# Depthwise-convolution taps, channel sums and buffer places rearranged in a one-core layer kernel

## The chip, the cores and the metric

One Trainium2 chip; the kernel runs on 1 core. The metric is the device time of one execution in microseconds. Before the change it is 2488.69 us, the median of 3 runs (2487.4 to 2490.93). TensorE (PE) multiplies, VectorE (DVE), ScalarE (ACT) and GpSimd (POOL) work on elements, SyncE (SP) issues most of the DMAs. PE takes weights and data from SBUF and writes to PSUM, which has eight banks of 128 x 512 floats here.

## The reference

One layer on 512 positions of width 2048, all in fp32. Two mixers share one normalised input h, then a gated merge and a small embedding step:

```
proj = h @ w_in                       # qkv, z_a, b, a, glu_in, z_b, gate_logits
o_a  = gated_delta(silu(conv4(qkv)))  # 16 heads of 128, chunks of 64: a triangular solve per chunk
y_a  = (rmsnorm(o_a) * silu(z_a)) @ w_br_a
u    = glu(glu_in)                    # first half * sigmoid(second half)
u    = causal_depthwise_conv(u, w_dw) + b_dw            # 31 taps for each of 2048 channels
y_b  = (silu(layernorm(u)) * silu(z_b)) @ w_br_b        # mean and variance over the channels
x    = x + rmsnorm((sigmoid(ga) * y_a + sigmoid(gb) * y_b) @ w_out)
x    = x + rmsnorm(sigmoid(x @ w_ple_gate) * (p @ w_ple_proj))
```

## The kernel before, in words

**Products.** Each fp32 operand is split into a high part (a cast, on ACT) and a low part (the difference, on DVE or POOL), and a product is three matmuls: high by high, high by low, low by high. A matmul here is 128 x 128 by 128 x 512. A weight piece is read from memory by SP into a raw tile (three buffers), cast (L126) and subtracted (L127) into a tile of the pool `ring` (four buffers, low in each SBUF partition). `low_part[0]` names the engine of L127: DVE at first, POOL from the end of the heads until the layer norm begins.

**Stages, in order of time.** The input is loaded, normalised and transposed. `z_phase` makes z and both gates with a Strassen-Winograd scheme: sums of weight blocks are formed by DVE and by accumulating DMAs that POOL issues, and the pieces (L404 to L414) lie by turns in `ring` and, every third, in two tiles of the pool `slots` (21 buffers of 2 KB, high in the partition). Then the heads: eight groups of two, each with six products for q, k and v (`gemm_cm`, 48 matmuls each at L183, L185, L187, with two PSUM banks in turn), then the gated delta rule, of which the last steps are a triangular solve on DVE (a product L846 and a reduction L847 in turn) and small matmuls (L748, L867) that wait for it. Then branch a (L1052, L1054, L1056 with oh and ol) alternates with the products of the gated linear unit: for each of the channel tiles 5 to 15 two products of 48 matmuls, and after each pair from 6 on a job of 48 matmuls of branch a. The layer norm over the channels follows beside the last jobs of branch a, then branch b (L1052 again, with uh and ul), then w_out by Strassen-Winograd (L1341 to L1343), and the embedding step.

**Background work.** Every matmul of `gemm_cm` and `branch` calls `tick()`. Generators are spawned with a period in ticks and step when it has passed: `group` for a head group, `convs` for the depthwise convolution, `split_oa` for the low parts `ol` of branch a (L1031), `layer_norm`. The order on each engine is fixed before the run by a scheduler that goes through the program with its own costs: an instruction is issued when its operands are ready and the buffer of its tile is free by those costs, the one that stands first in the program ahead of the others. Buffers of one tag are given in program order. On the chip each engine keeps to that order, and an instruction that has to wait holds up all behind it on its engine.

**The convolution.** For a tile of 128 channels `evac_glu_b` puts a sigmoid into the tile `sg`; `evac_glu_a` multiplies the other half of the unit by it (L943). Up to the end of the heads, channels 0 to 4, the product stays in `sg` (SBUF); after it a PSUM pool `ups` of two banks is open, and the product is written there (`up`). `dwconv` starts the sum of a channel on ACT (L919, `uc`) and does 30 taps on DVE (L922), one for each step of the generator, with period CP = 4. When they are done, POOL adds the channel to `acc` (L926, L928; its mean over channels opens the layer norm), and SP writes it to memory (L929). `convs` is spawned 288 matmuls before the end of the heads.

**w_out.** `run` takes two PSUM banks for each product from `bank()`: six of eight calls give one from the pool `fps` (f), two one from `gps` (g). The operands of w_out are formed at the same time by `split_mixed`, whose transposed tiles also lie in `gps` and are read last at L1225. With the counter at 0, P1, P7 and the second P1 get f f, f f, f g, and P2 g f.

Of the kernel before, what the change touches and what calls it, by code (L numbers as in the profile page):

```python
# [24 lines left out]
TAPS = 31  # L25
LOP = 23
HP = 4
CP = 4
QKV_TILES = 48
Z_TILE0 = 48  # L30
BA_TILE = 64
# [6 lines left out]
V_DW = V_CONV + QKV_TILES * 4  # L38
V_BDW = V_DW + NK * TAPS
# [41 lines left out]
def _body(ctx, tc, A, out):  # L81
    nc = tc.nc
# [25 lines left out]
    def vv(col, n=1):  # L108
        return vec[:, col:col + n]
# [31 lines left out]
    def spawn(gen, period, key=None):  # L141
        active.append([gen, period, period, key])
# [147 lines left out]
    B11, B12, B22, B21 = range(4)  # L290
    OPND = {"P1": "A11", "Q5": "S1", "P7": "S3", "P6": "S2", "P3": "S4", "P2": "A12", "Q4": "A22"}

    def stepper(gen, n=1):
        def f(k=None):
            for _ in range(n):
                next(gen, None)
        return f

    def z_phase():
        ctx_z = ExitStack()  # L300
        zs = ctx_z.enter_context(tc.tile_pool(name="zs", bufs=32))
        zps = ctx_z.enter_context(tc.tile_pool(name="zps", bufs=6, space=PSUM))
        S = {n: [None] * 4 for n in ("S1", "S2", "S3", "S4")}

        def tt_(dst, a, b, op):
            nc.vector.tensor_tensor(dst, a, b, op)
# [42 lines left out]
        WZ = {g: A["w_" + g] for g in ("z", "ga", "gb")}  # L349
        entries, sources, pieces = deque(), deque(), deque()  # L350
        tz = {}
        cnt = dict(load=0, piece=0)

        def load(grp, jp, blk, q):
            cnt["load"] += 1
            if cnt["load"] <= 4 or cnt["load"] % 5 in (2, 4):
                two = [slots.tile([P, T], F32, tag="s", name="zraw") for _ in range(2)]
                for n in range(2):
                    nc.sync.dma_start(two[n], WZ[grp][jp, blk, q][:, n * T:(n + 1) * T])
                return two  # L360
            raw = rawp.tile([P, 1024], F32, tag="raw", name="raw", bufs=3)
            nc.sync.dma_start(raw, WZ[grp][jp, blk, q])
            return [raw[:, 0:T], raw[:, T:]]

        def acc(t, grp, jp, blk, q):
            nc.gpsimd.dma_start(t, WZ[grp][jp, blk, q], accum_op=ALU.add)

        def parts(t):
            return [t[:, 0:T], t[:, T:]]

        def e_a(grp, jp, q):
            b11, b12 = load(grp, jp, B11, q), load(grp, jp, B12, q)
            tz[q] = zs.tile([P, 1024], F32, tag="t", name="zt", bufs=4)
            t = parts(tz[q])
            for n in range(2):
                tt_(t[n], b11[n], b12[n], ALU.add)
            return [b11, t]

        def e_b(grp, jp, q):
            b22, b12 = load(grp, jp, B22, q), load(grp, jp, B12, q)  # L380
            t = parts(tz[q])
            for n in range(2):
                tt_(t[n], t[n], b22[n], ALU.add)
                tt_(b12[n], b12[n], b22[n], ALU.add)
            return [t, b12, b22]

        def e_c(grp, jp, q):
            acc(tz[q], grp, jp, B21, q)
            return [load(grp, jp, B21, q), parts(tz[q])]

        for grp in WZ:
            for jp in range(2):
# [3 lines left out]
        def enter():  # L396
            e, *where = entries.popleft()
            for src in e(*where):
                sources.extend(src)

        def piece():
            while len(pieces) < 4 and (sources or entries):
                while len(sources) < 4 and entries:
                    enter()  # L404
                src = sources.popleft()
                cnt["piece"] += 1
                if cnt["piece"] % 3:
                    w = ring.tile([P, 1024], F32R, tag="w", name="w")
                    hi, lo = w[:, 0:T], w[:, T:]
                else:  # L410
                    hi, lo = [slots.tile([P, T], F32R, tag="s", name="zw") for _ in range(2)]
                nc.scalar.copy(hi, src)
                tt_(lo, src, hi.bitcast(F32), ALU.subtract)
                pieces.append((hi, lo))  # L414
            return pieces.popleft()

        def run(products, side=None):
            ps = {pr: [zps.tile([P, T], F32, tag="z", name="zp") for _ in range(2)] for pr in products}
            for q in range(4):
                for pr in products:  # L420
                    for n in range(2):
                        wh, wl = piece()
                        for t in range(2):
                            lh, ll = opnd(OPND[pr], 2 * q + n, t)
                            mm(ps[pr][t], lh, wh, start=q + n == 0, stop=False)  # L425
                            mm(ps[pr][t], ll, wh, start=False, stop=False)  # L426
                            mm(ps[pr][t], lh, wl, start=False, stop=q == 3 and n == 1)  # L427
                    if side:
                        side()
            return ps  # L430
# [22 lines left out]
        gen = form()  # L453
# [7 lines left out]
        for grp, jp in [(g, n) for g in WZ for n in range(2)]:  # L461
            rows = None if grp == "z" else bias_rows(grp, jp)
            ps = run(("P1", "Q5"), stepper(gen, 2))
# [8 lines left out]
            ps = run(("P6", "P7", "P3"))  # L472
# [11 lines left out]
            ps = run(("P2", "Q4"))  # L484
# [45 lines left out]
    u_dram = dram.tile([NK, P, T], F32, name="u_dram")  # L530
# [374 lines left out]
    cpool = [slots, "s"]  # L905
    ups = None
    waiting = deque()
# [5 lines left out]
            sg_t[i] = sg  # L913
        return f

    def dwconv(i, u):
        w0 = V_DW + i * TAPS
        y = cpool[0].tile([P, T], F32, tag=cpool[1], name="uc")
        nc.scalar.activation(y, u, AF.Identity, scale=vv(w0 + TAPS - 1), bias=vv(V_BDW + i))  # L919
        yield  # L920
        for s in range(1, TAPS):
            nc.vector.scalar_tensor_tensor(y[:, s:], u[:, 0:T - s], vv(w0 + TAPS - 1 - s), y[:, s:], ALU.mult, ALU.add)  # L922
            yield
        if i == 0:
            acc.append(slots.tile([P, T], F32, tag="s", name="acc"))
            nc.gpsimd.tensor_copy(acc[0], y)  # L926
        else:
            nc.gpsimd.tensor_tensor(acc[0], acc[0], y, ALU.add)  # L928
        nc.sync.dma_start(u_dram[i], y)  # L929
        done[0] += 1  # L930

    def convs():
        while done[0] < NK:
            if waiting:
                yield from dwconv(*waiting.popleft())
            else:
                yield

    def evac_glu_a(i):
        def f(ps):  # L940
            sg = sg_t.pop(i)
            u = ups.tile([P, T], F32, tag="u", name="up") if ups else sg
            nc.vector.tensor_tensor(u, ps, sg, ALU.mult)  # L943
            waiting.append((i, u))
        return f

    def glu_b(i):
# [57 lines left out]

    jobs.append(lambda: spawn(convs(), CP, "convs"))
    for i in range(2, 5):
# [10 lines left out]
    ups = s2_ctx.enter_context(tc.tile_pool(name="ups", bufs=2, space=PSUM))  # L1018
# [278 lines left out]
    def load(jp, pr, q):  # L1297
        n = loads[0]
        loads[0] += 1
        if n < 3 or n % 8 in (1, 4, 7):  # L1300
            raw = rawp.tile([P, 1024], F32, tag="raw", name="raw", bufs=3)
        else:
            raw = s3.tile([P, 1024], F32, tag="rw", name="rw", bufs=5)
        src, blk = WHICH[pr]
        nc.sync.dma_start(raw, src[jp, blk, q])
        sources.append(raw)
# [35 lines left out]
            mm(ps, ll, wh[:, c], start=False, stop=False)  # L1342
            mm(ps, lh, wl[:, c], start=False, stop=kk == 7)  # L1343

    banks = [0]

    def bank():
        banks[0] += 1
# [99 lines left out]
    fin = out_fin(0, gp)  # L1448
    ps = run(("P7",), stepper(gen, 2))
    s7 = [snap(SLOT, x) for x in ps["P7"]]  # L1450
    ps = run(("P1",), stepper(gen, 3))
    drain(gen)
    s1b = [snap(HP_, x) for x in ps["P1"]]
    ps = run(("P2",))
    for t in range(2):
        fin(t, 0, add(unit(S3_, "c11"), ps["P2"][t], s1[t]))
    ps = run(("Q5",))
    s5 = [snap(S3_, x) for x in ps["Q5"]]
    ps = run(("P6",))
# [28 lines left out]
    ps = run(("P7",), stepper(pgen))  # L1488
# [5 lines left out]
    ps = run(("Q4",), stepper(pgen, 3))  # L1494
# [81 lines left out]
    last = ple_last(bcast_row(A["g_ple"], 3))  # L1576
    for k in range(12, NK):
        hold(k)
    for tt in range(NTT):
        ps = bank()  # L1580
# [8 lines left out]
        for j in range(4):  # L1589
            s = e_t4[tt][j]  # L1590
# [67 lines left out]
```

## Time and profile before

| what | value |
|---|---|
| median of 3 runs | 2488.69 us (2487.4 to 2490.93) |
| the profiled execution | 2491.45 us, its span 2489.7 us |
| PE busy | 2431.6 us, 98% of the span |
| DVE, ACT, POOL busy | 1821.3, 1160.2, 426.5 us |
| mean granted clock of PE | 0.991 |
| head stage | some 590 to 1520 us |
| last tap of the convolution | ends at 1904.6 us |
| branch b, first matmul | 1949.96 us |

How to read it: an engine's busy time counts its instructions, not its waits. A wait of an engine is put down to the instruction that released it: "PE g L187 <- POOL w L127: 14.0, 1, 14.0" says that the matmul at L187 waited 14.0 us in total, once, 14.0 at most, until POOL's L127 had written w. Rows of a timeline give start, length, engine, line, operation, output and inputs, count, and in brackets the idle time ahead with what ended it. Groups give the count, the sum of busy time in us and the mean of one in ns. Matmuls overlap in the records, so their pitch is the distance between two starts. Stretches of 50 us give each engine's busy time in us and count, the granted clock of PE (1.00 is full), the share of time in which the DMA engines worked, and GB/s.

### The profile page before, as it was taken

What the parts mean: (1) busy time and instruction counts of PE and PEld (TensorE: products, weight loads), DVE (VectorE), ACT (ScalarE), POOL (GpSimd) and SP (SyncE); (2) the same over time, 40 slices, a digit from 0 to 9 for tenths busy, and PEclk for the clock granted to TensorE, in tenths of its full rate; (3) what the DMA queues carried; (4) which work ended last, traced back from release to release, by engine and by line L of the source; (5) the groups of instructions that cost most, each with busy time, mean ns of one, the idle gap of its engine ahead of it and who ended that gap; (6) DMA issues with size and microseconds to landing.
All of it is one profiled execution on the core that took longest, in us unless ns stands there. A gap on an engine that the chain in (4) does not pass through costs nothing. (4 is left out here: it accounts for less than half of the span.)

```text
span 2489.7 us, 33469 instructions
## 1 busy us (share of the span) xinstructions
PE 2431.6 (98%) x11962; PEld 1989.3 (80%) x11962; DVE 1821.3 (73%) x3401; ACT 1160.2 (47%) x2284; POOL 426.5 (17%) x451
## 2 busy tenths in 40 slices
PE   8999999999999999999999989799999999999998
PEld 7888888887888888888888867688888788788886
DVE  7878787877677676777767799978777854667644
ACT  6445444555555555555565534122223623444532
POOL 0000000012212112132200114445553000000000
PEclk9999999999999999999999999899999999999999
DMA  7567675766636354475622224233344543575542
GB/s 266 169 183 206 183 206 195 227 163 188 185 110 185 102 158 129 130 204 151 181 75 93 73 85 141 84 102 106 108 139 135 182 127 98 186 235 170 204 169 76
DMA packets 141831, 380.19 MB, mean 153 GB/s; under 512 B 15968, under 2 KB 24416, under 8 KB 141664
## 3 DMA queue, kind: packets, MB, share of 16 engines
q1 hardware_dynamic: 119008, 319.32, 38.5%
q0 software_dynamic: 20352, 54.54, 9.9%
q10 hardware_dynamic: 2304, 4.20, 0.5%
q8 instruction: 94, 1.54, 0.3%
q14 instruction: 73, 0.60, 0.1%
HBM read 329.75 MB, written 48.23 MB: 152 GB/s over the span
## 5 line engine op out<-in xcount | busy, mean ns | idle before, releaser
L126 ACT CAST w<-raw 128x512 fp32r<-128x512 f32 x588 | 359.1, 619 | 587.2 <-PE g L187 272.1
L187 PE MATMUL g<-hh,w 128*128 128x512 f32 x1536 | 611.4, 398 | 16.1 <-POOL w L127 14.0
L183 PE MATMUL g<-hh,w 128*128 128x512 f32 x1536 | 610.4, 397 | 2.8 <-DVE up L943 1.6
L185 PE MATMUL g<-hl,w 128*128 128x512 f32 x1536 | 611.4, 398 | 0.0
L127 DVE TENSOR_TENSOR w<-raw,w 128x512 fp32r<-128x512 f32 x444 | 307.3, 699 | 170.6 <-ACT w L126 168.3
L187 PEld LDWEIGHTS g<-hh,w 128*128 128x128 f32 x1536 | 289.8, 189 | 73.3 <-POOL w L127 14.4
L183 PEld LDWEIGHTS g<-hh,w 128*128 128x128 f32 x1536 | 289.9, 189 | 57.9 <-ACT w L126 3.0
L185 PEld LDWEIGHTS g<-hl,w 128*128 128x128 f32 x1536 | 289.8, 189 | 56.1 <-issue 1.5
L922 DVE SCALAR_TENSOR_TENSOR uc<-up,vec,uc 128x505 f32<-128x505 f32 (+18 forms) x330 | 233.2, 731 | 52.8 <-ACT uc L919 45.5
L127 POOL TENSOR_TENSOR w<-raw,w 128x512 fp32r<-128x512 f32 x144 | 193.9, 1349 | 221.4 <-ACT w L126 216.2
L922 DVE SCALAR_TENSOR_TENSOR uc<-sg,vec,uc 128x508 f32<-128x508 f32 (+20 forms) x150 | 128.2, 881 | 0.6
L660 DVE SCALAR_TENSOR_TENSOR cv<-g,vec,cv 128x511 f32<-128x511 f32 x144 | 106.3, 738 | 27.3 <-ACT cv L658 26.8
L1052 PE MATMUL yp<-w,uh 128*128 128x512 f32 x256 | 101.3, 396 | 4.6 <-ACT uh L1140 4.6
L1056 PE MATMUL yp<-w,ul 128*128 128x512 f32 x256 | 101.1, 396 | 0.0
L1054 PE MATMUL yp<-w,uh 128*128 128x512 f32 x256 | 101.0, 395 | 0.0
L426 PE MATMUL zp<-w,zol 128*128 128x512 f32 x256 | 100.4, 392 | 0.0
L1054 PE MATMUL yp<-w,oh 128*128 128x512 f32 x256 | 99.7, 390 | 0.5 <-POOL w L127 0.5
L1052 PE MATMUL yp<-w,oh 128*128 128x512 f32 x256 | 100.1, 391 | 0.0
L425 PE MATMUL zp<-w,zoh 128*128 128x512 f32 x256 | 99.9, 390 | 0.0
L427 PE MATMUL zp<-w,zoh 128*128 128x512 f32 x256 | 99.7, 389 | 0.0
L1056 PE MATMUL yp<-w,ol 128*128 128x512 f32 x256 | 99.6, 389 | 0.0
L846 DVE TENSOR_TENSOR prod<-UT,VT 128x2 f32<-128x2 f32 (+30 forms) x248 | 87.7, 354 | 5.8
(384 smaller groups left out, 4713.9 us busy)
## 6 DMA issues: line engine op xcount, KB each, us to landing
raw<-in_w_in SPq DMA_DIRECT2D x194, 512.0 KB, 3.4
wsum<-in_w_out POOLq DMA_DIRECT2D x96, 256.0 KB, 5.1
raw<-in_w_ple_gate SPq DMA_DIRECT2D x40, 512.0 KB, 4.2
wo_sums<-wsum POOLq DMA_DIRECT2D x64, 256.0 KB, 4.0
raw<-in_w_br_a SPq DMA_DIRECT2D x32, 512.0 KB, 3.3
raw<-in_w_br_b SPq DMA_DIRECT2D x32, 512.0 KB, 3.3
raw<-in_w_ga SPq DMA_DIRECT2D x24, 512.0 KB, 4.4
raw<-in_w_gb SPq DMA_DIRECT2D x24, 512.0 KB, 4.4
```

Source lines behind the costliest of these rows:

```text
L126: nc.scalar.copy(hi, rq)
L127: low_part[0].tensor_tensor(lo, rq, hi.bitcast(F32), ALU.subtract)
L183: mm(ps, wh, rh, start=(k == 0), stop=False)
L185: mm(ps, wh, rl, start=False, stop=False)
L187: mm(ps, wl, rh, start=False, stop=(k == NK - 1))
L425: mm(ps[pr][t], lh, wh, start=q + n == 0, stop=False)
L426: mm(ps[pr][t], ll, wh, start=False, stop=False)
L660: nc.vector.scalar_tensor_tensor(y[:, s:], ps[:, 0:T - s], vv(w0 + 3 - s), y[:, s:], ALU.mult, ALU.add)
L922: nc.vector.scalar_tensor_tensor(y[:, s:], u[:, 0:T - s], vv(w0 + TAPS - 1 - s), y[:, s:], ALU.mult, ALU.add)
L1052: mm(ps[tt], lh[:, b], wh, start=k == 0, stop=False)
L1054: mm(ps[tt], lh[:, b], wl, start=False, stop=False)
L1056: mm(ps[tt], ll[:, b], wh, start=False, stop=k == NK - 1)
```

## The change

Four things change.

- The convolution. Its period before the heads end is 10 ticks for a tap instead of 4; once `ups` is open a tap takes 3 and 4 ticks in turn. The product of the linear unit always goes into `sg` in SBUF. `near()` prepares the next channel at tap 24 of the current one: once `ups` is open it copies the product to a PSUM tile on ACT, and it starts the sum on ACT. The channel's addition to `acc` is written at tap 18 of the next channel (`filtered`), its DMA to memory stays behind its last tap.
- The block sums `zt` of the z phase move from four tiles of 4 KB in the pool `zs` to eight of 2 KB in `slots`, with two accumulating DMAs of 256 KB in place of each of 512 KB.
- Weight pieces of the z phase lie by turns in `ring` and in a new pool `zw` of four buffers, opened ahead of `zs`, low in the partition; none lies in `slots`.
- In w_out the bank counter starts at -1: P1, P7 and the second P1 get f f, P2 gets g g. The operands' generator is stepped with 2 instead of 3 during the second P1.

```diff
-CP = 4
+CP = 10
...
+        zw = ctx_z.enter_context(tc.tile_pool(name="zw", bufs=4))
         zs = ctx_z.enter_context(tc.tile_pool(name="zs", bufs=32))
...
         def acc(t, grp, jp, blk, q):
-            nc.gpsimd.dma_start(t, WZ[grp][jp, blk, q], accum_op=ALU.add)
+            for n in range(2):
+                nc.gpsimd.dma_start(t[n], WZ[grp][jp, blk, q][:, n * T:(n + 1) * T], accum_op=ALU.add)
...
-            tz[q] = zs.tile([P, 1024], F32, tag="t", name="zt", bufs=4)
-            t = parts(tz[q])
+            t = tz[q] = [slots.tile([P, T], F32, tag="s", name="zt") for _ in range(2)]
...
-                if cnt["piece"] % 3:
-                    w = ring.tile([P, 1024], F32R, tag="w", name="w")
-                    hi, lo = w[:, 0:T], w[:, T:]
-                else:
-                    hi, lo = [slots.tile([P, T], F32R, tag="s", name="zw") for _ in range(2)]
+                w = ring.tile([P, 1024], F32R, tag="w", name="w") if cnt["piece"] % 2 else zw.tile([P, 1024], F32R, tag="zw", name="zw")
+                hi, lo = w[:, 0:T], w[:, T:]
...
+    def filtered(i, y):
         if i == 0:
             acc.append(slots.tile([P, T], F32, tag="s", name="acc"))
             nc.gpsimd.tensor_copy(acc[0], y)
         else:
             nc.gpsimd.tensor_tensor(acc[0], acc[0], y, ALU.add)
-        nc.sync.dma_start(u_dram[i], y)
         done[0] += 1
 
+    def near():
+        if not waiting:
+            return None
+        i, u = waiting.popleft()
+        if ups:
+            up = ups.tile([P, T], F32, tag="u", name="up")
+            nc.scalar.copy(up, u)
+            u = up
+        y = cpool[0].tile([P, T], F32, tag=cpool[1], name="uc")
+        nc.scalar.activation(y, u, AF.Identity, scale=vv(V_DW + i * TAPS + TAPS - 1), bias=vv(V_BDW + i))
+        return i, u, y
+
+    def pace(s):
+        return (3 + s % 2) if ups else CP
+
     def convs():
+        ready = last = None
         while done[0] < NK:
-            if waiting:
-                yield from dwconv(*waiting.popleft())
-            else:
-                yield
+            ready = ready or near()
+            if not ready:
+                if last and last[0] == NK - 1:
+                    filtered(*last)
+                yield 1
+                continue
+            (i, u, y), ready = ready, None
+            w0 = V_DW + i * TAPS
+            for s in range(1, TAPS):
+                nc.vector.scalar_tensor_tensor(y[:, s:], u[:, 0:T - s], vv(w0 + TAPS - 1 - s), y[:, s:], ALU.mult, ALU.add)
+                if s == 18 and last:
+                    filtered(*last)
+                    last = None
+                if s == 24:
+                    ready = near()
+                yield pace(s)
+            nc.sync.dma_start(u_dram[i], y)
+            last = i, y
...
-            u = ups.tile([P, T], F32, tag="u", name="up") if ups else sg
-            nc.vector.tensor_tensor(u, ps, sg, ALU.mult)
-            waiting.append((i, u))
+            nc.vector.tensor_tensor(sg, ps, sg, ALU.mult)
+            waiting.append((i, sg))
...
-    banks = [0]
+    banks = [-1]
...
-    ps = run(("P1",), stepper(gen, 3))
+    ps = run(("P1",), stepper(gen, 2))
     drain(gen)
```

More of the change, by code (lines that the diff above doesn't have):

```diff
@@ L365, in acc @@
         def acc(t, grp, jp, blk, q):
-            nc.gpsimd.dma_start(t, WZ[grp][jp, blk, q], accum_op=ALU.add)
-        def parts(t):
-            return [t[:, 0:T], t[:, T:]]
+            for n in range(2):
+                nc.gpsimd.dma_start(t[n], WZ[grp][jp, blk, q][:, n * T:(n + 1) * T], accum_op=ALU.add)
         def e_a(grp, jp, q):
             b11, b12 = load(grp, jp, B11, q), load(grp, jp, B12, q)
-            tz[q] = zs.tile([P, 1024], F32, tag="t", name="zt", bufs=4)
-            t = parts(tz[q])
+            t = tz[q] = [slots.tile([P, T], F32, tag="s", name="zt") for _ in range(2)]
             for n in range(2):
@@ L380, in e_b @@
             b22, b12 = load(grp, jp, B22, q), load(grp, jp, B12, q)
-            t = parts(tz[q])
+            t = tz[q]
             for n in range(2):
@@ L388, in e_c @@
             acc(tz[q], grp, jp, B21, q)
-            return [load(grp, jp, B21, q), parts(tz[q])]
+            return [load(grp, jp, B21, q), tz[q]]
         for grp in WZ:
@@ L914, in evac_glu_b @@
         return f
[L916 to L919, printed above, removed]
-        yield
-        for s in range(1, TAPS):
-            nc.vector.scalar_tensor_tensor(y[:, s:], u[:, 0:T - s], vv(w0 + TAPS - 1 - s), y[:, s:], ALU.mult, ALU.add)
-            yield
+    def filtered(i, y):
         if i == 0:
@@ L928, in dwconv @@
             nc.gpsimd.tensor_tensor(acc[0], acc[0], y, ALU.add)
-        nc.sync.dma_start(u_dram[i], y)
         done[0] += 1
+    def near():
[11 more added lines that the diff above has]
+        return (3 + s % 2) if ups else CP
     def convs():
+        ready = last = None
         while done[0] < NK:
-            if waiting:
-                yield from dwconv(*waiting.popleft())
-            else:
-                yield
+            ready = ready or near()
[16 more added lines that the diff above has]
+            last = i, y
     def evac_glu_a(i):
```

## The prediction, made before the changed kernel was run

> **What bounds the kernel now.** I read the page's first part, then what TensorE (PE) waited for, then the 50-us stretches around each wait, and the rows of the engine named.
>
> ```profile
> PE 2431.6 (98%) x11962; PEld 1989.3 (80%) x11962; DVE 1821.3 (73%) x3401; ACT 1160.2 (47%) x2284; POOL 426.5 (17%) x451
> ```
>
> PE is busy for 98% of the span and the change takes no matmul away. So only three things can be won: PE's waits, time at a lowered clock, and the pitch of a matmul. The waits of PE that touch the change (total, times, longest, us):
>
> ```profile
> PE g L187 <- POOL w L127: 14.0, 1, 14.0
> PE py L867 <- DVE Tc L861: 4.9, 1, 4.9
> PE yp L1052 <- ACT uh L1140: 4.6, 1, 4.6
> PE f L1341 <- DVE sf L1225: 4.4, 1, 4.4
> PE po L748 <- DVE O L743: 2.5, 2, 1.4
> PE g L183 <- DVE up L943: 1.6, 1, 1.6
> ```
>
> The stretches that hold them (busy time and count of PE, weight load, DVE, ACT, POOL; granted clock; DMA share; GB/s):
>
> ```profile
> 1450.00:1500.00 50.00, 43.19 (x267) 32.64 (x266) 44.70 (x91) 18.96 (x43) 7.46 (x5) 0.90 0.22 69
> 1550.00:1600.00 50.00, 35.98 (x153) 29.40 (x152) 49.82 (x59) 9.18 (x15) 20.55 (x14) 0.87 0.25 85
> 1900.00:1950.00 50.00, 45.20 (x200) 36.20 (x198) 37.65 (x65) 23.66 (x39) 8.18 (x7) 0.99 0.44 149
> 1950.00:2000.00 50.00, 50.00 (x210) 40.70 (x211) 40.09 (x67) 26.90 (x45) 0.00 (x0) 0.95 0.48 162
> 2150.00:2200.00 50.00, 45.55 (x193) 37.04 (x192) 33.34 (x43) 27.13 (x37) 0.00 (x0) 0.93 0.64 220
> ```
>
> A wait of 4.4 us or more is followed by a lowered clock. One minus the clock, times 50 us, is what it costs beyond the wait: 5.0, 6.5, 0.5 + 2.5 = 3.0, and 3.5 us. With it the four places cost 9.9, 20.5, 7.6 and 7.9 us.
>
> **Why GpSimd (POOL) is late by 14 us.** From the heads' end on it makes the weights' low parts (L127) and adds each convolved channel to the sum (L928). Its rows, then DVE's for the taps, and DVE's groups, the first two of them in 1520 to 1650 us:
>
> ```profile
> 1593.59 1.68 POOL L928 TENSOR_TENSOR acc<-acc,uc 128x512 f32<-128x512 f32 x1 [19.90 <-DVE uc L922]
> ```
> ```profile
> 1553.55 18.72 DVE L922 SCALAR_TENSOR_TENSOR uc<-sg,vec,uc 128x507 f32<-128x507 f32 x17
> 1572.79 26.30 DVE L922 SCALAR_TENSOR_TENSOR uc<-sg,vec,uc 128x497 f32<-128x497 f32 x35
> 1604.55 19.91 DVE L922 SCALAR_TENSOR_TENSOR uc<-up,vec,uc 128x507 f32<-128x507 f32 x26
> ...
> L922 DVE SCALAR_TENSOR_TENSOR uc<-sg,vec,uc 128x491 f32<-128x491 f32 (+22 forms) x70 | 66.4, 1000 | 0.2
> L922 DVE SCALAR_TENSOR_TENSOR uc<-up,vec,uc 128x511 f32<-128x511 f32 (+29 forms) x60 | 44.0, 733 | 2.3 <-ACT uc L919 0.4
> L1031 DVE TENSOR_TENSOR ol<-oa,oh 128x512 fp32r<-128x512 f32 x16 | 14.6, 915 | 0.0
> L943 DVE TENSOR_TENSOR up<-g,sg 128x512 f32<-128x512 f32 x11 | 7.6, 691 | 1.3 <-PE g L187 1.1
> ```
>
> The sum stands at the head of POOL's queue and waits 19.9 us for a tap, with low parts behind it. PE got 19.9 − 14.0 = 5.9 us further on pieces already prepared. The taps are late because one that reads u from SBUF (sg) while POOL works comes every 18.72/17 = 1.10 us; with POOL quiet every 26.30/35 = 0.75; from PSUM (up) every 19.91/26 = 0.77 with POOL at work. The excess is 70 × (1.000 − 0.733) = 18.7 us, and 16 × (0.915 − 0.691) = 3.6 us for the low parts ol: 22.3, about the 19.9 seen.
>
> The Trainium skill agrees ("SBUF — State Buffer", section "SBUF: two separate sides"): a DVE operation with two SBUF inputs and a GpSimd one that reads SBUF exclude each other for a whole instruction. A rule speaks against the change: "VectorE: DVE Perf Modes", "Rules for kernel authors", advises a copy from PSUM to SBUF where many operations follow, and this kernel will do the opposite. By it the copies would only cost; the rows, 0.75 quiet from SBUF against 0.77 from PSUM, leave it nothing to save and show it 0.33 worse beside POOL.
>
> **The parts, with gains positive.**
>
> *Sums and taps.* Channels 2 to 15 will be read from PSUM, so of 70 stretched taps at most channel 1's 30 remain: 30 × 0.267 + 3.6 = 11.6 us, scaled by 19.9/22.3 to 10.4, less the 5.9 of cover: a wait of 4.5 and some 3.4 of clock, together 8 at worst; nothing if that channel is done before POOL takes the low parts. That the sum is written a channel later I count as nothing: where the scheduler issues an operation as soon as it thinks it ready, its place in the queue stays. I take half, 4: gain 20.5 − 4 = **16.5** (0 if the queue is as before, to 20.5). The accumulation per channel and its DMA stay one each.
>
> *The copies to PSUM.* 14 more on ACT, with a cast as the nearest row:
>
> ```profile
> L126 ACT CAST w<-raw 128x512 fp32r<-128x512 f32 x588 | 359.1, 619 | 587.2 <-PE g L187 272.1 <-PE yp L1056 203.6 <-PE f L1509 42.5
> L919 ACT ACTIVATE uc<-up,vec 128x512 f32<-128x512 f32 x11 | 8.5, 782 | 0.3 <-DVE up L943 0.3
> ```
>
> 14 × 0.62 = 8.7 us, hidden: ACT is busy for 47% of the span, and for 9.2 of 50 us in the stretch from 1550. A copy waits for the PSUM buffer of the channel before last, and weight casts queue behind it; it is issued 24 taps after that buffer's last reader, so 24 × 0.77 = 18 us of lateness are covered. Without the cover each costs 0.6. The GLU product no longer waits for such a buffer: the 1.6 us at L943, which held PE's bank, go: **1.6** (0 to 2.5).
>
> *Sparse taps before the heads' end.* A tap per 10 matmuls, not 4. It is not the pace alone that places them:
>
> ```profile
> 1419.22 0.15 DVE L846 TENSOR_TENSOR prod<-UT,VT 128x2 f32<-128x2 f32 x1
> 1419.29 0.73 DVE L922 SCALAR_TENSOR_TENSOR uc<-sg,vec,uc 128x499 f32<-128x499 f32 x1
> 1419.95 0.15 DVE L847 TENSOR_REDUCE VT<-prod 128x1 f32<-128x2 f32 x1
> ...
> 1438.51 0.28 DVE L846 TENSOR_TENSOR prod<-UT,VT 128x60 f32<-128x60 f32 x1
> 1438.82 0.22 DVE L847 TENSOR_REDUCE VT<-prod 128x4 f32<-128x60 f32 x1
> ```
>
> Taps fill each gap of the last solve, and stretch a product-to-reduce step from 0.31 to 0.73 us. If all went, the waits at L867 and L748 would: 9.9 + 2.5 = 12.4. But channel 0 is ready as before, and only channel 1, whose start I expect some 8 us later in a solve of about 30 us from there, thins out: a quarter, **3** (−3, if SBUF slots run short, to 12.4).
>
> *Layer norm.* Its end of the chain:
>
> ```profile
> 1857.05 9.32 DVE L922 SCALAR_TENSOR_TENSOR uc<-up,vec,uc 128x511 f32<-128x511 f32 x12 [9.09 <-ACT uc L919]
> 1866.29 0.69 DVE L943 TENSOR_TENSOR up<-g,sg 128x512 f32<-128x512 f32 x1
> 1866.88 27.28 DVE L922 SCALAR_TENSOR_TENSOR uc<-up,vec,uc 128x499 f32<-128x499 f32 x41
> 1899.31 5.26 DVE L922 SCALAR_TENSOR_TENSOR uc<-up,vec,uc 128x488 f32<-128x488 f32 x7
> 1949.96 0.79 PE yp L1052
> ```
>
> The last tap ends at 1904.57, and branch b starts 45.4 us later, 4.6 after PE was ready for it (1945.4). Channel 15's product comes at 1866.3, when 18 taps of channel 14 are still to do; at 30 × 3.5 = 105 matmuls a channel against 144 between products, channel 14 will be done. Then copy 0.6, start 0.8 and 30 × 0.77 = 23 put the last tap 25 us after the product instead of 38: 13 us won against 4.6 missing. Gain **7.6** (−10 to 7.6, the third rival).
>
> *z and gates.* Start-to-start of 6 matmuls on a piece in two high tiles (zw), then 12 on ring pieces:
>
> ```profile
> 304.40 0.39 PE L425 MATMUL zp<-zw,hh 128*128 128x512 f32 x1
> 305.80 0.39 PE L425 MATMUL zp<-w,hh 128*128 128x512 f32 x1
> 308.54 0.39 PE L425 MATMUL zp<-zw,hh 128*128 128x512 f32 x1
> ```
>
> 233 against 228 ns; 3 × 128 + 3 × 96 = 672 such matmuls: **3.4** (0, if the pitch isn't the address's, to 3.4). The block sums now take eight of the 21 slots, in which loads and results of this stage live too, and each accumulating DMA becomes two on POOL's queue, which works at nothing else there: 24 issues more. One row of the page gives a load's time to landing:
>
> ```profile
> raw<-in_w_ga SPq DMA_DIRECT2D x24, 512.0 KB, 4.4
> ```
>
> No wait of PE in this stage is over 1 us, so loads are ahead; a load that found no slot could cost its 4.4 us once, which would turn the 3.4 into −1.
>
> *w_out's banks.*
>
> ```profile
> 2163.54 0.39 PE L1343 MATMUL f<-wsp,ah 128*128 128x512 f32 x1
> 2168.38 0.77 PE L1341 MATMUL f<-wsp,ah 128*128 128x512 f32 x1 [4.45 <-DVE sf L1225]
> ...
> 2167.81 0.76 DVE L1225 TENSOR_TENSOR sf<-tp,sf 128x256 f32<-128x256 f32 x2
> ```
>
> The second half of P1 waits for a bank that L1225 still reads. With both banks in the other pool, 24 matmuls × 0.227 = 5.4 us can run before P2 needs it; it was short by 4.45, so 0.95 is to spare. The mix's steps come closer together (every second call, not every third), but two weight splits of 1.22 each could now come ahead of L1225:
>
> ```profile
> 2158.37 1.22 DVE L1323 TENSOR_TENSOR wsp<-rw,wsp 128x1024 fp32r<-128x1024 f32 x1 [0.82 <-ACT wsp L1322]
> ```
>
> That would leave 1.5 us of wait, too short to lower the clock; I take off half. Gain 7.9 − 0.8 = **7.1** (0, where P2 waits instead, to 7.9).
>
> Sum: 16.5 + 1.6 + 3 + 7.6 + 3.4 + 7.1 = 39.2. The profiled run took 2491.45 (span 2489.7, 1.75 around it), so 2452.3; the median shown is 2.8 lower: 2449.5, **2450 us**. Its own range, 2441 to 2459, is the widest term's way to its end (heads, 9.4) to either side.
>
> **Rivals.** *Heads freed:* the solve runs without taps and POOL never waits: 9.4 + 4 more, **2436**. For: taps visibly stretch the solve. Against: channel 0's are ready all the same. *POOL waits as before:* the sum keeps its place and channel 1 is as late: 2450 + 16.5 = **2466**. Against: 40 of 70 stretched taps go. *DVE is full:* with some 40 taps done by the heads' end (1520.7 − 6.4 = 1514.3), 440 remain, and 14.6 + 7.6 + 8.2 (12 gate products like L943's) = 30.4 of other work. At 0.766 a tap the last ends at 1514.3 + 337 + 30.4 = 1882, branch b can start at 1927, and PE is there at 1945.4 − 24.5 = 1921: a wait of 6 and 3.4 of clock, **2460**; with gaps like the 9.09 above up to 2470. Against: two channels side by side take 27.28/41 = 0.665. *Slower:* the same sum with slower taps. Each 0.01 us a tap costs 4.4; all 39.2 are spent when branch b starts at 1921 + 39.2 − 3.4 = 1957, the last tap ends at 1911 and a tap takes 0.83. At 0.849, the mean of the 130 taps in the two rows of 1520 to 1650, it waits till 1964: 43 + 3.4, **2496**. For: ACT now writes one PSUM buffer while DVE reads the other. Against: no PSUM tap of before shows it, though ACT started channels from there too.
>
> **How the numbers follow.** Forecast 0.42, heads freed 0.20, DVE full 0.17, POOL as before 0.08, slower 0.08, no change 0.05 (gains spent on waits not named). Within 0.2%, 5 us, is what can't be told from none. Faster 0.87, same 0.05, slower 0.08. The range, 2432 to 2474, takes in all but the last two and the edges.
>
> **What would show it.** POOL's longest wait for L922 at 5 to 10 us, not 19.9; taps from up near 0.73 us x420 or so; no wait at L1341 for L1225 and a clock of 1.00 after 2150; none at L1052 for uh. Wrong if PE waits for ACT's copy, or if DVE stays at 49 of 50 us till 1880.

## The result, and the profile after

The changed kernel takes 2465.8 us (median of 4 runs, 2461.44 to 2467.9) against 2489.81 before in the same session: 24 us less, a ratio of 0.99 with an interval of 0.9882 to 0.9919. Forecast were 2450 (2432 to 2474): the direction and the range held, and 24 of the 39 us came. The profiled execution took 2465.07 us, 26.4 less than the one of before.

The waits of PE in the changed kernel that answer to those shown of before:

```profile
PE yp L1068 <- DVE gt L1080: 9.1, 2, 7.3
PE py L862 <- DVE Tc L856: 7.4, 1, 7.4
PE po L743 <- DVE O L738: 1.9, 2, 1.0
PE f L1357 <- ACT wsp L1338: 1.7, 1, 1.7
```

and its stretches of 50 us (columns as before):

```profile
1450.00:1500.00 50.00, 45.04 (x290) 35.73 (x291) 40.78 (x86) 21.91 (x57) 5.51 (x4) 0.84 0.20 67
1500.00:1550.00 50.00, 48.15 (x209) 39.20 (x208) 45.55 (x64) 23.75 (x49) 27.94 (x21) 0.97 0.49 162
1550.00:1600.00 50.00, 50.00 (x222) 41.42 (x221) 49.26 (x75) 14.15 (x23) 26.80 (x21) 1.00 0.34 113
...
1900.00:1950.00 50.00, 42.72 (x176) 34.26 (x177) 40.98 (x67) 29.52 (x47) 0.00 (x0) 0.93 0.53 185
```

Three things are to be seen. PE's wait for POOL is gone altogether, and 1550 to 1600 is full at a clock of 1.00. The wait for the last solve (L862, before at L867) has grown from 4.9 to 7.4 us, and the clock around it is lower: (1 − clock) x 50 is 8.0 + 1.5 us in the two rows, against 5.0. And branch b, which waited 4.6 us for uh, now waits 7.3 us for gt, in a row with a clock of 0.93.

Where the time was won can be read off two places that every kernel here has, with the same number of PE's matmuls ahead of them (7982 and 9626): the first matmul of branch a (with oh) and that of branch b (with uh). The range in each row is the start of the first and of the last; before, then after:

```profile
L1052 PE MATMUL yp<-w,oh x256: 387/389/791, 1552.4 to 1943.2; 128*128 128x512 f32 x128
L1052 PE MATMUL yp<-w,uh x256: 387/389/793, 1950.0 to 2132.2; 128*128 128x512 f32 x128
```
```profile
L1068 PE MATMUL yp<-w,oh x256: 387/389/793, 1546.1 to 1921.4; 128*128 128x512 f32 x128
L1068 PE MATMUL yp<-w,uh x256: 387/389/766, 1929.6 to 2111.2; 128*128 128x512 f32 x128
```

The z phase's last matmul starts at 558.1 us before and at 550.9 after, 7.2 earlier. From there to branch a it takes 994.3 us before and 995.2 after, 0.9 more. From branch a's first matmul to branch b's it takes 397.6 and 383.5, 14.1 less. What follows adds 6.0, nearly all of it in w_out.

POOL's two longest waits for a tap, and DVE's groups, all in the changed kernel:

```profile
1556.09 1.30 POOL L916 TENSOR_TENSOR acc<-acc,uc 128x512 f32<-128x512 f32 x1 [2.29 <-DVE uc L946]
1571.28 1.30 POOL L916 TENSOR_TENSOR acc<-acc,uc 128x512 f32<-128x512 f32 x1 [3.89 <-DVE uc L946]
...
L946 DVE SCALAR_TENSOR_TENSOR uc<-up,vec,uc 128x491 f32<-128x491 f32 (+27 forms) x420 | 290.9, 732 | 16.1 <-ACT uc L928 7.1 <-POOL w L127 1.6
L946 DVE SCALAR_TENSOR_TENSOR uc<-sg,vec,uc 128x511 f32<-128x511 f32 (+29 forms) x60 | 46.3, 772 | 0.5
L1047 DVE TENSOR_TENSOR ol<-oa,oh 128x512 fp32r<-128x512 f32 x16 | 18.1, 1185 | 0.0
```

A tap from PSUM takes 0.732 us with POOL at work, as before. Only 60 taps read SBUF, and 52 of them start ahead of POOL's first low part (at 1483.0); POOL's longest wait for a tap is 3.89 us where it was 19.90, and 5 to 10 were forecast.

### The profile page after: what moved, and what is told of

Same layout as the page of the kernel before. It is cut to its first block, busy times and chain, and to the rows that moved or that the text cites. A ratio compares the mean times of both kernels' runs of the same rounds, so it can differ in the third digit from the quotient of the medians.

```text
span 2463.3 us, 33657 instructions
## 1 busy us (share of the span) xinstructions
PE 2421.1 (98%) x11962; PEld 1990.4 (81%) x11962; DVE 1812.4 (74%) x3409; ACT 1175.0 (48%) x2298; POOL 432.1 (18%) x467
## 4 chain that ended last, share of the span: by engine, by line
PE 90%; DVE 6%; ACT 2%; issue 1%; DMA 1%; POOL 0%; SPq 0%; DVEq 0%; POOLq 0%; ACTq 0%
PE g L185 13%; PE g L187 13%; PE g L183 13%; PE zp L422 6%; PE zp L421 6%; PE zp L420 6%; PE yp L1068 4%; PE yp L1072 4%; PE yp L1070 4%; PE f L1357 2%; PE f L1358 2%; PE f L1359 2%; PE f L1525 2%; PE f L1524 2%; PE f L1523 2%
## 5 line engine op out<-in xcount | busy, mean ns | idle before, releaser
L127 DVE TENSOR_TENSOR w<-raw,w 128x512 fp32r<-128x512 f32 x452 | 312.4, 699 | 179.0 <-ACT w L126 176.8
L946 DVE SCALAR_TENSOR_TENSOR uc<-up,vec,uc 128x491 f32<-128x491 f32 (+27 forms) x420 | 290.9, 732 | 16.1 <-ACT uc L928 7.1
L127 POOL TENSOR_TENSOR w<-raw,w 128x512 fp32r<-128x512 f32 x136 | 179.0, 1317 | 256.3 <-ACT w L126 252.1
L984 POOL DMA_DIRECT2D wsum<-in_w_out x96 | 75.5, 837 | 69.8 <-DMA wsum<-in_w_out 35.8
L1357 PE MATMUL f<-wsp,oph 128*128 128x512 f32 x192 | 75.5, 393 | 1.7 <-ACT wsp L1338 1.7
L1523 PE MATMUL f<-w,xh 128*128 128x512 f32 x192 | 75.4, 393 | 0.0
L1358 PE MATMUL f<-wsp,opl 128*128 128x512 f32 x192 | 75.2, 392 | 0.0
```

The costliest lines, as they stand in the source:

```text
L127: low_part[0].tensor_tensor(lo, rq, hi.bitcast(F32), ALU.subtract)
```

## The experiments

### The parts alone

The kernel before with one part of the change at a time: the whole new z phase (`b_z`), the bank counter and stepper (`b_banks`), and the new convolution with its period (`b_conv`).

```diff
 b_z:      + the new z_phase (pool zw, zt in slots, two accumulating DMAs)
 b_banks:  -    banks = [0]              +    banks = [-1]
           - stepper(gen, 3) in the second P1   + stepper(gen, 2)
 b_conv:   + filtered, near, pace, convs, evac_glu_a of the change, CP = 10
```

> The kernel before with the z phase of the changed kernel alone. Theory: the gain of this part is the pitch of its matmuls, and it is larger than the 3.4 us forecast, since in the profile after the ring pieces too come every 227 ns: the heads start some 7 us earlier, so 2483 us against 2490. Rival as forecast: only the 672 matmuls of the high pieces gain, 3.4 us, 2486. Rival: the eight slots make loads late, 2490 or more.

> The kernel before with the bank counter and the stepper of the changed kernel alone. Theory: the wait of 4.4 us at L1341 for L1225 and the lowered clock behind it go, and about 2 us of short waits stay: 6 us, 2484 against 2490. Rival: P2 waits for the same reader instead, 2490.

> The kernel before with the changed convolution alone (period 10, copies to PSUM, sums a channel late). Theory: 21 us from POOL's wait and its clock and 3 at L943, less 4 at the last solve and 4 at branch b: 2474 against 2490. If the three parts do not add up to the whole change (24 us), one of them hangs on another.

Measured: `b_z` 2483.68 us (ratio 0.9975, 0.9964 to 0.9985), `b_banks` 2484.47 (0.9978, 0.9968 to 0.9988), `b_conv` 2474.73 (0.9939, 0.9927 to 0.9951), all against 2490.3. The gains are 6.6, 5.8 and 15.6 us, 28 in all; the whole change gives 24. The runs of one kernel lie some 5 us apart, so this says that the parts add up roughly, and no more.

In the stretch from 150 to 350 us, where PE never waits, the count of matmuls shows the z part. Before, then `b_z`:

```profile
150.00:350.00 200.00, 200.00 (x871) 162.92 (x870) 157.93 (x255) 99.72 (x172) 7.92 (x9) 1.00 0.69 199
```
```profile
150.00:350.00 200.00, 200.00 (x884) 165.58 (x883) 162.11 (x260) 103.13 (x175) 17.80 (x20) 1.00 0.70 204
```

884 against 871 in 200 us is 1.5% more. 2016 matmuls of the stage at 0.23 us are 460 us, so 6.8 us. The stage's last matmul starts 6.8 us earlier too (551.3 against 558.1): the whole gain is pitch, and the loads from 8 fewer slots are not late.

### Where the piece lies: its place or its two tiles

`b_z` left open why a piece in the slots is slower. Two kernels, both of them `b_z` with one edit: the pool zw at the other side of SBUF, from byte 149,376 of the partition on; and zw low, but high and low part in a tile each, as they were in the slots.

```diff
 b_zhigh: -tc.tile_pool(name="zw", bufs=4)   +tc.tile_pool(name="zw", bufs=4, side="right")
 b_ztwo:  -    w = ... zw.tile([P, 1024], F32R, ...)
          +    hi, lo = [zw.tile([P, T], F32R, tag="zw", name="zw") for _ in range(2)]      # bufs=8
```

> The kernel before with the z phase of the changed kernel, its new pool zw put on the other side of SBUF, from byte 149,376 of the partition on instead of 83,072. Theory: the pitch of a matmul hangs on the address of its moving piece; every second piece then lies high, the pitch there is 233 ns as for pieces in the slots, and 1008 of 2016 matmuls lose 6 to 7 ns each, so the gain of 6.6 us is gone: 2489 to 2491. Rival: it is the two separate tiles for high and low part that cost, or the bound lies above 160,000: 2483.

> The kernel before with the z phase of the changed kernel, but each piece of zw in two tiles of 2 KB (one for the high, one for the low part, eight buffers) in place of one of 4 KB, at the same low place. With zw high (from 149,376 on) its matmuls came every 227 ns all the same. Theory: the pitch of 233 ns belongs to the slots' place, above 165,952; here it stays 227, and the time is that of the z part alone, 2484. Rival: it comes from keeping high and low part in two tiles; the pitch of zw's matmuls is 233 again, and the time 2489.

Measured: `b_zhigh` 2485.7 us against 2488.1 (0.9984, 0.9975 to 0.9993), `b_ztwo` 2482.35 against 2489.01 (0.9974, 0.9965 to 0.9983). The first theory of the two fell in its form. The stretch of `b_zhigh`, then of `b_ztwo`:

```profile
150.00:350.00 200.00, 200.00 (x884) 165.65 (x883) 161.16 (x259) 102.27 (x173) 17.80 (x20) 1.00 0.71 204
```
```profile
150.00:350.00 200.00, 200.00 (x883) 165.41 (x882) 159.03 (x256) 100.97 (x171) 16.61 (x19) 1.00 0.71 204
```

Both have the quick pitch. Two tiles don't cost anything, and neither does a place from 149,376 up. What is left is the slots' own place, from 165,952 up, or something else that lies with these buffers; no run here put a piece of zw above 165,952 in a pool of its own, so the last step is argued. (The places are worked out from the sizes of the pools; no trace shows an address.) `b_zhigh` gained less for another reason: its z phase ends as early (550.6), but a wait behind it, of 0.7 us in the changed kernel, is longer here:

```profile
PE sw_ps L613 <- ACT ba_s L609: 2.4, 1, 2.4
```

### The copies to PSUM

```diff
-        if ups:
-            up = ups.tile([P, T], F32, tag="u", name="up")
-            nc.scalar.copy(up, u)
-            u = up
```

> The changed kernel without the copies to PSUM: all taps read u from SBUF, everything else as it is. Theory: beside POOL's low parts a tap then takes some 1.0 us on average instead of 0.73, 420 x 0.27 = 113 us more for DVE than it has room for; POOL's sums wait again, and the kernel is 60 to 130 us slower than the changed one. Rival: DVE has enough idle time to hide it, less than 20 us slower.

Measured: 2567.46 us (ratio to before 1.0312, 1.0296 to 1.0327), 102 us slower than the changed kernel. Its taps and its waits:

```profile
L942 DVE SCALAR_TENSOR_TENSOR uc<-sg,vec,uc 128x493 f32<-128x493 f32 (+18 forms) x480 | 464.7, 995 | 11.7 <-POOL acc L916 1.9 <-POOL w L127 0.9
...
PE yp L1066 <- POOL w L127: 42.7, 6, 12.5
PE g L187 <- POOL w L127: 27.9, 5, 8.4
PE sum_ps L1114 <- POOL acc L916: 10.3, 1, 10.3
```

A tap takes 0.995 us against 0.732, and PE pays for it in eleven waits for POOL's low parts where before had two, of 14.0 and 0.5. The 60 taps that read SBUF in the changed kernel, most of them ahead of POOL's turn, took 0.772, which points to POOL's work beside them. The copies are what this part of the change lives on. The Trainium skill offers a copy from PSUM to SBUF ahead of many operations ("VectorE: DVE Perf Modes", "Rules for kernel authors"); here, beside POOL, the opposite copy pays. Its page "SBUF — State Buffer" ("SBUF: two separate sides") states that a DVE operation with two SBUF inputs and a GpSimd one that reads SBUF lock each other out for a whole instruction, and these times agree with it.

### The sum a channel later

```diff
-                if s == 18 and last:
-                    filtered(*last)
-                    last = None
...
-            last = i, y
+            filtered(i, y)
```

> The changed kernel with the channel's sum written right after its last tap, not a channel later. Theory: the queue's order goes by readiness and the taps are no longer late, so this makes no difference: within 4 us of the changed kernel, POOL's waits for taps below 10 us in total. Rival: writing the sum later is what freed POOL, and the wait of 14 us and its clock come back, 15 to 21 us slower than the changed kernel.

Measured: 2463.61 us (0.9899, 0.9884 to 0.9913), the same as the changed kernel within the spread of its runs. PE's longest waits are the same (7.3 for gt, 7.3 at py); POOL waits 6.7 us for taps in total against 9.2. Writing the sum later moves nothing that counts, as it must be if the scheduler issues it when it thinks it ready.

### How sparse the taps should be

First with the old period, then with no tap ahead of the heads' end.

```diff
 a_cp4:    -CP = 10
           +CP = 4
 a_notaps: -    jobs.append(lambda: spawn(convs(), CP, "convs"))
           ...
                low_part[0] = nc.gpsimd
           +    spawn(convs(), CP, "convs")
```

> The changed kernel with a period of 4 for the taps until the heads end, as before. Theory: the wait at the last solve (py for Tc) does not come from the number of taps; DVE is late there because it waited 4 us for ACT's copies Ud, and the solve's own steps add to it where no tap fills them. So dense taps make it shorter again, about 5 us instead of 7.4, and the kernel 2 to 5 us faster than the changed one, unless the taps then left make the convolution end earlier or later: 2461 to 2466. Rival: the sparse taps were a gain, and with 4 the kernel is 5 us or more slower than the changed one, 2471.

> The changed kernel with the convolution spawned behind the heads' end: no tap runs before it. Theory: with no taps the last solve is shorter, but PE still comes to py before Tc is there, or does so no more only because py stands behind other matmuls in the program; the lateness of DVE against PE in the solve (4 us from Ud, growing in steps without taps) stays. The convolution starts 60 taps later and its end 30 us or more later, so branch b waits that long less its margin: 15 to 40 us slower than the changed kernel. Rival: the taps are what makes the solve late, the wait at py goes, and the kernel is not slower.

Measured: `a_cp4`, with 87 taps ahead of the heads' end in place of 60, 2472.99 us (0.9932, 0.9919 to 0.9944), 7 slower than the changed kernel; `a_notaps` 2439.0 (0.9793, 0.9777 to 0.981), 27 faster than the changed kernel and 51 faster than before. Both went against the theory under test, that the number of taps doesn't matter to the wait at py. The waits of `a_cp4`, then of `a_notaps`:

```profile
PE g L183 <- DVE sg L959: 6.1, 1, 6.1
...
PE po L743 <- DVE O L738: 3.4, 4, 1.5
PE py L862 <- DVE Tc L856: 1.9, 1, 1.9
```
```profile
PE po L743 <- DVE O L738: 3.1, 4, 1.0
PE yp L1068 <- ACT uh L1156: 2.6, 2, 1.9
PE f L1357 <- ACT wsp L1338: 1.7, 1, 1.7
```

With a period of 4 the wait at py is indeed short, as expected; but a new one of 6.1 us stands behind the heads, where a product (L959) is late in a DVE queue full of taps and low parts ol. Without taps neither is there. The stretches from 1450 to 1550 in `a_notaps`:

```profile
1450.00:1500.00 50.00, 46.79 (x263) 38.34 (x258) 28.41 (x72) 25.90 (x71) 11.13 (x10) 1.00 0.18 64
1500.00:1550.00 50.00, 50.00 (x222) 41.38 (x222) 50.00 (x72) 19.00 (x33) 26.33 (x20) 1.00 0.42 147
```

The clock stays at 1.00, where the changed kernel's two rows show 0.84 and 0.97. But the heads are not all of the 27 us. The first matmuls of the two branches in `a_notaps`:

```profile
L1068 PE MATMUL yp<-w,oh x256: 389/389/791, 1531.1 to 1903.9; 128*128 128x512 f32 x128
L1068 PE MATMUL yp<-w,uh x256: 387/389/499, 1906.6 to 2087.1; 128*128 128x512 f32 x128
```

Against the changed kernel's profiled execution it is 15.0 us ahead at branch a, 23.0 at branch b and 24.1 at the end. So some 15 us belong to the heads; most of the rest is branch b's wait, 9.1 us for gt in the changed kernel and 2.6 for uh here, with its clock. `a_cp4` is 5.7 us behind at branch a (1551.8) and no more than that at the end. How the solve stands to PE, in DVE's last row of Tc and PE's first of py, in the changed kernel and in `a_notaps`:

```profile
1455.46 0.44 DVE L856 STREAM_TRANSPOSE Tc<-VP 32x256 f32<-32x256 f32 x1 [0.23 <-ACT VP L855]
1454.02 0.28 PE L862 MATMUL py<-Tc,W 32*32 32x32 f32 x2 [7.40 <-DVE Tc L856]
```
```profile
1441.92 0.44 DVE L856 STREAM_TRANSPOSE Tc<-VP 32x256 f32<-32x256 f32 x1 [0.27 <-ACT VP L855]
1444.36 0.69 PE L862 MATMUL py<-Tc,W 32*32 32x32 f32 x32
```

Tc ends 13.5 us earlier without taps, and py starts 2.0 us behind it without a wait. DVE waits for ACT's Ud at the start of this solve in both kernels and starts its first product at nearly the same time (1411.7 and 1412.0), so it is not that DVE comes into it earlier.

The other half of the expectation failed too: the end of the convolution is not later. All 480 taps, started at 1495.1, end at 1864.3; in the changed kernel 420 are left for the time from 1522.8, and the last ends at 1866.6. DVE is full from 1500 to 1550, catches up, and from 1602 on the waits of its taps are for a channel's start (uc).

### The place of py

```diff
-        yield 22
+        yield 22 if g < NH // 2 - 1 else 58
         pz = wps.tile([P, 8, 64], F32, tag="w", name="pz")
```

> The changed kernel with the products py and pz of the last group written 36 matmuls (8.2 us) later behind its solve. My first theory of the wait at py (it does not hang on the taps) has fallen: without taps it is gone. The new one: the taps make the solve so long that the scheduler places py right behind it, with no cover, and PE then waits for whatever DVE is later on the chip than planned (4 us from Ud, 7 at the end). With 8.2 us of matmuls between, the wait of 7.4 and its clock (8) shrink to under 2: 2450 to 2458, less what these matmuls then lack as filling behind the heads. Rival: only the length of the solve counts, the last steps of the heads come later by what py waits less, and nothing is gained: 2463 to 2470.

Measured: 2462.2 us (0.989, 0.9875 to 0.9906), 3.6 faster than the changed kernel: inside the spread, and inside the rival's numbers. Its waits:

```profile
PE psB L708 <- DVE VP L883: 4.8, 1, 4.8
PE po L743 <- DVE O L738: 4.0, 3, 2.1
...
PE py L862 <- DVE Tc L856: 1.3, 2, 1.0
```

The wait at py is gone, as the theory had it, and comes back at the next two places where PE needs DVE. So cover at one step is not enough here. Taking the taps out makes the chain of the last heads as a whole shorter, and that won the time.

### What branch b waits for

The last loop of the layer norm, 16 channels, spread out from 8 to 12 matmuls a channel.

```diff
         for i in range(NK):
             u = u_t[i]
             nc.vector.tensor_tensor(u, u, rstd, ALU.mult)
...
-            yield
+            yield 6
...
-            yield
+            yield 6
```

> The changed kernel with the last loop of the layer norm spread out (12 matmuls a channel, the pace at which branch b uses them, instead of 8). Theory: branch b waits 7.3 us for the products gt of branch a's last tiles because these stand behind the layer norm's last steps in DVE's queue, not because the layer norm is late; spread out, gt comes earlier, the wait shrinks below 2 us and with it the clock's 3.4: 7 to 9 us faster than the changed kernel. Rival: the layer norm itself is late (DVE is full), and branch b then waits for uh: no faster, or slower.

Measured: 2456.43 us (0.9867, 0.9852 to 0.9881), 9.4 faster than the changed kernel, as the theory had it. DVE's queue in the changed kernel around the end of branch a (PE stands from 1922.3 on), then PE's one wait of this kind in `a_ln` with its stretch:

```profile
1921.52 1.89 DVE L1158 TENSOR_TENSOR ul<-ur,uh 128x512 fp32r<-128x512 f32 x3
1923.32 1.29 DVE L127 TENSOR_TENSOR w<-raw,w 128x512 fp32r<-128x512 f32 x2
1924.53 1.88 DVE L1149 TENSOR_TENSOR ur<-ur,rstd_ps 128x512 f32<-128x512 f32 x3
1926.32 1.89 DVE L1154 TENSOR_TENSOR ur<-ur,zb 128x512 f32<-128x512 f32 x3
1928.13 0.68 DVE L1158 TENSOR_TENSOR ul<-ur,uh 128x512 fp32r<-128x512 f32 x1
1928.73 0.68 DVE L1080 TENSOR_TENSOR gt<-yp,gt 128x512 f32<-128x512 f32 x1
```
```profile
PE yp L1068 <- DVE gt L1080: 1.8, 1, 1.8
...
1900.00:1950.00 50.00, 49.71 (x218) 40.42 (x217) 43.51 (x74) 32.70 (x51) 0.97 (x1) 1.00 0.63 219
```

From 1922.3 to 1928.7 DVE works at steps of the layer norm and two low parts of weights (L127), while PE's next matmul waits for the product gt behind them, which frees branch b's PSUM banks. By the scheduler's rule those steps stand ahead because they come first in the program and were ready. With the loop spread out, gt comes through in time.

### Both together

> The changed kernel with the convolution spawned behind the heads' end and the last loop of the layer norm spread out. Theory: the first alone gave 2439; of the waits left there only the 2.6 us at uh touch the layer norm's end, and spreading it cannot make uh earlier: 2437 to 2441. Rival: the two gains add (27 and 9 us), 2430.

The two edits, taps after the heads and the loop spread out, give 2438.75 us (0.9798, 0.9783 to 0.9813; against 2488.1): as fast as without the second, 49 us under before in the medians. In `a_notaps` the convolution's last tap ends 40 us before PE is through with branch a, and 56 us before in the changed kernel, so the layer norm comes later against PE; the first gt (1902.97) stands behind only two steps of its last loop, and there is nothing left for the second edit to win. Either kernel beats both of the kernels compared here.

## Why the prediction was right or wrong

By its own terms, in us. The first two rows and the fourth are read from waits and from the stretch between the two branches, the third from the stretch between the z phase and branch a; the last two are the kernel with that part alone.

| term | forecast | measured | from |
|---|---|---|---|
| sums and taps (POOL) | 16.5 | 15.7 | a wait of 14.0 and 1.7 of clock behind it, all gone |
| product L943 | 1.6 | 1.6 | gone |
| heads' end | 3 | −0.9 | 994.3 before, 995.2 after |
| layer norm and branch b | 7.6 | −3.2 | what is left of the 14.1 between the branches: 14.1 − 15.7 − 1.6 |
| z and gates | 3.4 | 6.6 | `b_z` |
| w_out's banks | 7.1 | 5.8 | `b_banks` |
| sum | 39.2 | 25.6 | the medians give 24.0, the profiled executions 26.4 |

*The price of the clock* was wrong. I took (1 − clock) x 50 as a cost beyond the wait. But the clock falls while PE still stands, and what is lost then costs nothing more. Before, in POOL's wait and in the 4 us behind it:

```profile
1583.00:1597.00 14.00, 0.04 (x1) 0.04 (x1) 13.93 (x20) 0.19 (x1) 3.41 (x3) 0.64 0.05 19
1597.00:1601.00 4.00, 4.00 (x11) 3.16 (x12) 3.96 (x5) 0.00 (x0) 3.24 (x2) 0.57 0.37 131
```

(1 − 0.64) x 14 = 5.0 us of what I had read as 6.5 lie inside the wait, and only (1 − 0.57) x 4 = 1.7 behind it. The place cost 15.7 us, not 20.5. At the shorter waits less is counted twice: at w_out 2.7 us of the 3.5 lie behind the wait.

*POOL's wait* was understood: its cause and its going. That 16.5 came so close is luck. I took 4 us off for channel 1's taps beside POOL, which cost nothing, as most of these were done before POOL took over; and the price from which I took them was 4.8 too high. The working that gives 22.3 us of stretched taps and low parts is generous too: it goes by mean lengths of records that overlap, and by busy time (66.4 / 70 = 0.949 a tap) it is 15.1 + 3.6 = 18.7, against the 19.9 seen. That the sum's place in the program would do nothing was right (`a_prompt`).

*Layer norm* failed in a step, not a size. That the convolution would end some 13 us earlier against PE was right: its last tap ended 40.7 us before PE was through with branch a (1904.6 against 1945.3), and now ends 55.7 us before (1866.6 against 1922.3), 15 earlier. But I let the whole wait vanish with it, and didn't ask what is late next. The layer norm that starts earlier puts its last steps into DVE's queue ahead of gt; `a_ln`, which only spreads these steps out, is 9.4 us faster, so it is this order and not DVE's load. I had forecast "none at L1052 for uh", which came true, and a saving, which did not. By waits and the clock behind them the place cost 4.6 + 2.7 before and 9.1 + 2.2 after, 4.0 more.

*Heads' end*: "a quarter" of 12.4 did not come; nothing was won. The stretch from the z phase to branch a takes 994.3 us before and 995.2 after, and 993.2 in `b_conv` and 992.3 in `a_prompt`, which have the same heads, the same wait at py and less of a lowered clock behind it. The reasoning that a sparse period leaves channel 0's taps where they are was right: 60 taps still lie ahead of the heads' end, against 80. What failed is the step from a shorter solve to a shorter wait. The last solve did get shorter, from 49.8 us (1419.2 to 1469.0, first product to last reduction) to 39.5 (1411.7 to 1451.2). But so did the stretch of matmuls that the scheduler planned beside it: 47 fewer lie ahead of py, some 10.7 us at 0.227, and PE met py that much earlier. PE stood idle for 10.1 us between 1400 and 1540 before and for 10.5 after. The wait at one place is not what the taps cost: `a_cp4` has the short wait at py and is slower, `a_py` moves the wait on. In the changed kernel 87, 60 and no taps there give 2473, 2466 and 2439 us, of the last step some 15 us in the heads. The rival "heads freed" had the mechanism right, and its 2436 is near what `a_notaps` reaches; that the numbers meet is in part luck, as it prices the clock as I did and z at half. The period of 10 only does not bring it about.

*z* was half the size: I counted the 672 matmuls on high pieces and took the ring's 228 ns as given. After the change every matmul of the stage comes at 227, the ring's too.

*The banks* were 1.3 over: 4.4 us of wait and 2.7 of clock behind it went, and a wait of 1.7 us for a weight split stays at L1357. It is of the kind that I had taken half of, but it is one on ACT.

*DVE is full* didn't happen, not even with 480 taps behind the heads (`a_notaps`): taken over all of it, (1864.3 − 1495.1 − 30.4)/480 is 0.706 us a tap, near the 0.665 of two channels side by side, and well under the 0.766 of the rival. *Slower* with taps from PSUM made slower by ACT's writes: 0.732 with the copies, no trace of it.

## What to carry to other kernels

Where each engine keeps a fixed order, a wait that goes is only won if what stands next in that queue was not needed sooner; read the queue behind the wait (here layer-norm steps ahead of the product that frees PSUM banks) before counting the gain. Count a lowered clock only from the wait's end on: at POOL's wait that left 1.7 us. To see where time was won, compare the times of matmuls that have the same work ahead of them. Background work in a dependent chain's gaps is not free when PE comes to wait for the chain: thinning it out (80 taps to 60) won nothing there, taking it out won some 15 us. Where two engines slow each other at SBUF, a copy of the operand that is read thirty times to PSUM, 0.59 us on an engine with time to spare, saved 102 us.

## What the runs showed of the hardware that was not expected

The pitch of matmuls that read pieces from the slots (165,952 up in the partition) is 233 ns; from a pool at 83,072 or at 149,376 it is 227, in one tile or in two, and the pieces in the ring between them get quicker too, from 228 to 227. Why is open.

The clock's loss does not follow from the length of the wait. The 7.4 us at the solve go with 8.0 + 1.5 us of (1 − clock) x 50 in the changed kernel, and with 5.0 + 1.5 in `b_conv`, where the wait and the heads' program are the same. A wait of 1.8 us in branch a leaves the clock at 1.00 in the changed kernel (1850 to 1900) and at 0.97 in `b_conv`. Nor does a busy PE bring it back at once. `b_conv`, then the changed kernel behind the wait at the solve, where PE works without a gap, mostly at matmuls of 32 or 64 rows (96 of the 112), and the clock stays near a half for 13 us:

```profile
1450.00:1500.00 50.00, 41.83 (x278) 32.80 (x277) 44.89 (x89) 19.66 (x50) 4.24 (x3) 0.90 0.20 64
1500.00:1550.00 50.00, 47.99 (x215) 38.93 (x216) 43.52 (x68) 25.31 (x54) 26.19 (x20) 0.97 0.50 166
```
```profile
1454.00:1467.00 13.00, 12.98 (x112) 9.53 (x113) 6.85 (x12) 5.18 (x11) 0.00 (x0) 0.52 0.12 42
```

Whether small matmuls keep the clock down was not tried on its own.

DVE's low parts ol, which read two SBUF tiles, still suffer beside POOL: 1.185 us each after the change and 0.915 before, against 0.69 for a product that reads PSUM.
